# A decoder trunk in exact f32: both column pairs of the MLP's last down group by seven products

## The chip, the cores and the metric

The kernel is one program on one core of a Trainium2 chip. The metric is the device time of one execution in microseconds (us), lower being better. The profile is one execution taken by the hardware profiler; its engines are PE (TensorE), DVE (VectorE), ACT (ScalarE), POOL (GpSimd) and SP (SyncE), the last issuing most transfers.

## The reference

`x` is 256 tokens by 2048. Layer 0 has differential attention, layer 1 latent attention; each is followed by attention into 256 memory tokens and by a squared-ReLU MLP with 8192 hidden columns:

```
def sq_relu_mlp(h, wup, wdown):
    return jnp.square(jax.nn.relu(h @ wup)) @ wdown
...
        a = (p[:, :, 0] - lam * p[:, :, 1]).astype(v.dtype)
        return jnp.einsum('bhqk,bkhd->bqhd', a, v)
...
    for i in range(DEPTH):
...
        x = x + sq_relu_mlp(rms_norm(x, mlp_norm[i]), mlp_wup[i], mlp_wdown[i])
    return rms_norm(x, final_norm)
```

`wup` is 2048 x 8192 and `wdown` 8192 x 2048 in each layer; everything is float32. `a` is the difference of two softmaxes (the second function above stands in the differential attention).

## The kernel before

**Weights.** A weight tile is 128 x 2048 floats (1 MB) and covers 512 rows by 512 columns of a matrix. A plain load puts it into one of seven `raw` tiles. TensorE's fast format holds fewer bits than a float, so each tile is split in two halves of 128x1024: ScalarE casts `raw` to `whi` (line 211), VectorE takes the difference `wlo` (line 212). Four such halves exist at a time, each a pair of `whi` and `wlo`. Activations are split in the same way. Each product is then three matmuls: high by high, low weight by high activation, high weight by low activation (line 164).

**Items.** The MLP's work on TensorE is a list of items. An ordinary *unit* uses one weight tile for both token tiles of 128: 24 matmuls of 128x512 that add into two PSUM banks `mm`. A *chunk* is a list of units with the same output columns; its sums are then added to `x` (line 515) or become hidden values. Hidden columns come in 8 blocks of 1024 (two halves of 512), and a down *group* b multiplies hidden block b with its rows of `wdown`; the output has four column chunks c = 0 to 3.

**Seven products.** A 2 x 2 block product over two token tiles, two weight halves and two column chunks takes eight half-units of 12 matmuls, or seven products p1 to p7 of 12 (banks `pr`), with sums of weight tiles and of activations in place of the eighth. `Seven` does the up projection so for hidden blocks 1 to 7, two depth steps each, 14 items per block. Weight sums are made by VectorE over whole raw tiles (line 837, 42 per layer) and by accumulating transfers of GpSimd (line 829, 14 per layer). `Final` does columns (2, 3) of the last down group by seven products, with two VectorE sums (line 952) and two accumulating transfers (line 949); columns (0, 1) there are four ordinary units. `Pair`, a subclass, does the same for the differential attention's output weights `da_wo` and makes all its weight sums by accumulating transfers, four for each pair.

**Order.** `mlp_line` (line 1089) writes the order of items. It mixes the 98 items of `Seven` with units of the down groups, by estimated VectorE and TensorE cost, into `line` (98 and 64 units in each layer), and sets `end` behind it: the last group, four units and `Final`'s seven products. A job (load and split) runs four items ahead of its matmuls. TensorE's order is that of the program. Around it the code inserts side tasks (softmax, transposes, norms) after a count of TensorE time that a step asks for with `yield`. The orders of VectorE, ScalarE, GpSimd and SP are set by a scheduler. In the differential attention such a step asks for `T_SM + 6.3 + slack` between the softmax of a block and the transposes of `a`, with a slack per head group.

A *seam* below is the place where the MLP's last results are transposed for the next layer's normed input.

Of the kernel before, what the change touches and what calls it, by code (L numbers as in the profile page):

```python
# [17 lines left out]
P = 128  # L18
D = 2048
S = 256  # L20
NT = 2
# [4 lines left out]
MLP_BLOCKS = 8  # L26
SEVEN = (1, 2, 3, 4, 5, 6, 7)
EVS = 7

# [18 lines left out]
def trunk(ctx, tc, x, xT, xT0, mem, memT, positions, gcols, gfinal, lam_vecs, consts, W, out):  # L48
# [121 lines left out]
    def f32(ap):  # L170
        return ap.bitcast(F32)
# [16 lines left out]
    def raw_tile():  # L188
        return wraw.tile([P, 4 * CH], F32, tag="raw", name=nm("raw"))
# [601 lines left out]
    def plan_mlp(l):  # L791
        plan.extend(j for line in mlp_lines[l] for item in line for j in item.jobs)
# [130 lines left out]
    class Final:  # L923

        ORDER = "p1 p2 p5 p6 p3 p7 p4".split()

        def __init__(self, l):
            self.l, self.b = l, MLP_BLOCKS - 1  # L930
            self.cols = (2, 3)
            self.raw = {}
            self.banks = {}
            self.parts = {}
            self.forms = {}

        def source(self, key):
            return W[f"mlp_wdown{self.l}"][8 * self.b + 2 * (1 + key % 10) + key // 10 - 1]

        def fetch(self, key):  # L940
            self.raw[key] = raw_tile()
            load(self.raw[key], self.source(key))

        def home(self, key):
            self.raw[key] = f32(unit()).rearrange("p a k t -> p (a k t)")
            return self.raw[key]

        def onto(self, o, key):
# [5 lines left out]
        def early(self):  # L954
            return [
                lambda hid: (
                    self.sums([k for c in range(2) for k in hid[self.b, c].tasks]),
                    self.fetch(11), load(self.home("t1"), self.source(11)),
                ),
                lambda hid: (self.onto("t1", 12), self.fetch(22), self.fetch(21)),  # L960
                lambda hid: (self.sum("t2", "t1", 22), self.sum("t4", "t2", 21)),
                lambda hid: self.fetch(12),
                lambda hid: self.onto(12, 22),
            ]

        def job(self, p):
            source = {"p1": 11, "p2": 21, "p3": 22, "p4": "t4", "p5": "t1", "p6": "t2", "p7": 12}[p]
            return lambda: halves_of(self.raw[source])

        def items(self):  # L970
            return [Item(self, p, [self.job(p)]) for p in self.ORDER]

# [26 lines left out]
        def products(self, inputs, p, nxt):  # L999
# [21 lines left out]
            for t, j, op in {  # L1021
                "p1": ((0, 0, ALU.add),), "p5": ((1, 1, ALU.add),), "p6": ((0, 1, ALU.subtract),), "p3": ((0, 1, ALU.add),),
                "p7": ((1, 1, ALU.subtract), (1, 0, ALU.add)), "p2": ((0, 0, ALU.add),), "p4": ((1, 0, ALU.add),),
            }[p]:
                xc = xs[t][:, self.cols[j] * CH : (self.cols[j] + 1) * CH]
                with urgent(), behind(added and p == "p7" and added[-1]):
                    summed = nc.vector.tensor_tensor(xc, xc, o, op)
                if p == "p4":
                    added.append(summed)
            done = {"p2": (2, 0), "p3": (3, 0), "p7": (3, 1), "p4": (2, 1)}  # L1030
            if nxt and p in done:
                nxt(*done[p], o)

    class Pair(Final):

        ORDER = "p1 p2 p5 p3 p6 p7 p4".split()
        FETCH = {"p1": ((11, 11), ("t", 12)), "p2": ((21, 21),), "p3": ((22, 22),)}
        STEP = {"p1": ("t", 11), "p5": ("t", 22), "p3": (22, 12), "p6": ("t", 21)}  # L1040
        SPLIT = {"p1": 11, "p2": 21, "p5": "t", "p3": 22, "p6": "t", "p7": 22, "p4": "t"}

        def __init__(self, name, first, cols, forms):
            self.name, self.first, self.cols, self.forms = name, first, cols, forms
            self.raw = {}
            self.banks = {}
            self.parts = {}
            self.steps = []
            self.splits = []

        def source(self, key):
            return W[self.name][4 * self.cols[key % 10 - 1] + self.first + key // 10 - 1]

        def part(self, t, c):
            if not self.parts:
                store = f32(unit()).rearrange("p a k (h t) -> p a (k h) t", t=P)
                self.parts = {(i, j): store[:, i, 4 * j : 4 * j + 4] for i in range(NT) for j in range(2)}
            return self.parts[t, c]

        def job(self, p):  # L1060
            def run():
                for key, at in self.FETCH.get(p, ()):
                    self.raw[key] = raw_tile()
                    load(self.raw[key], self.source(at))
                before = {"p5": ["p1"], "p6": ["p1", "p5"], "p7": ["p3"], "p4": ["p1", "p5", "p6"]}.get(p, [])
                assert all(i in self.steps for i in before)
                self.splits.append(p)
                return halves_of(self.raw[self.SPLIT[p]])

            return run  # L1070

        def items(self, inputs):
            return [Woven(self, p, inputs) for p in self.ORDER]

    class Woven:
# [3 lines left out]
        def step(self):  # L1079
            if self.p in self.of.STEP:  # L1080
                after = {"p5": "p5", "p3": "p3", "p6": "p6"}.get(self.p)
                assert after is None or after in self.of.splits
                self.of.onto(*self.of.STEP[self.p])
                self.of.steps.append(self.p)

        def emit(self):
            self.of.products(self.inputs, self.p, None)

    def mlp_line(l):
# [11 lines left out]
        def down(i):  # L1101

            end = len(groups) - 1
            pairs = ((0, 1), (2, 3)) if (end - i) % 2 == 0 else ((2, 3), (0, 1))
# [21 lines left out]

        rest, after = rest[:-3], rest[-3:]
# [17 lines left out]
        end = down(len(groups) - 1)  # L1145
        for item, step in zip(after + end, end[-1].of.early()):
            item.early = step
        return line + after, end
# [3 lines left out]
    def plan_woven(units, jobs):  # L1152
# [6 lines left out]
    da_pairs = [Pair("da_wo", 0, (c, c + 1), forms) for c in (0, 2)]  # L1159
# [3 lines left out]
        [of.job(p) for of in da_pairs for p in of.ORDER],  # L1163
# [198 lines left out]
    def attention(project, attend, mid, gcol, pairs=()):  # L1362
# [6 lines left out]
        for gi in range(4):  # L1369
# [5 lines left out]
            if pairs and gi == 2:  # L1375
                pairs[0].sums([k for i in first for k in i.tasks])
                weave.extend(k for of in pairs for k in of.items(first))
# [27 lines left out]
    def mlp(l, norm, gnext):  # L1405
# [8 lines left out]
        def out(b, c, t, src, r, wait):  # L1414
# [5 lines left out]
            def task():  # L1420
# [13 lines left out]
        def finish_chunk(of, ps, nxt):  # L1434
            for t in range(NT):
# [3 lines left out]
                else:  # L1439
                    add_residual(t, of.c, ps[t])  # L1440
                    if nxt is not None:
                        nxt(of.c, t, ps[t])
# [6 lines left out]
        def run(line, nxt=None):  # L1449
            for item in line:  # L1450
# [9 lines left out]
                if isinstance(of, Final):  # L1460
                    of.products([hid[of.b, c] for c in range(2)], item.u, nxt)
                    continue
# [10 lines left out]
                if item.u == n - 1 and of.close:  # L1473
                    finish_chunk(of, sums.pop((of.kind, of.c)), nxt)

        line, end = mlp_lines[l]
# [4 lines left out]
        def last(nxt):  # L1481
            free_banks[0] += limit
            run(end, nxt)
# [33 lines left out]
    da_slacks = [0.0, 0.0, 2.0, 0.0]  # L1517
# [298 lines left out]
```

## Time and profile before

| | |
|---|---|
| median of 3 runs | 2211.06 us (2210.5 to 2211.48) |
| the profiled execution's own time | 2209.08 us |
| its span | 2207.3 us |
| mean granted TensorE clock | 0.998 |
| matmuls on TensorE (page) | 10511 |
| VectorE instructions (page) | 2025 |

A group's row gives line, engine, operation, output<-inputs and count; then busy time and mean nanoseconds of one; then the idle time right before them and what ended most of it. A waits row gives the total, how many, and the longest. A row of a window gives its length and each engine's busy time with instruction counts, then the clock, the share of the transfer engines and GB/s. A row in time gives start and duration in us, and in brackets the idle time before it. Matmuls overlap: one of 128x512 lasts 0.39 us, and the next starts 0.23 us after it.

### The profile page before, as it was taken

To read this page: it belongs to the slowest core of one execution; us is meant where nothing else is said; L and a number is where in the kernel's file an instruction comes from. 1 tells how busy PE (TensorE), PEld (TensorE's weight loads), DVE (VectorE), ACT (ScalarE), POOL (GpSimd) and SP (SyncE) were. 2 spreads that over 40 slices of the span, in tenths; PEclk is the share of its full clock that TensorE was granted. 3 is DMA by queue.
4 is the path that set the end of the run, shared out by engine and by line. 5 is a ranking of instruction groups with operands and counts; after the bars stand their busy time and mean duration, and the time that the engine had idled before them with its cause. 6 is when DMAs were issued, how large, how long until landed. Compare 5 with 4: busy or idle time off the path is not lost.

```text
span 2207.3 us, 27663 instructions
## 1 busy us (share of the span) xinstructions
PE 2191.9 (99%) x10511; PEld 1838.4 (83%) x10511; DVE 1814.2 (82%) x2025; ACT 1388.1 (63%) x1855; POOL 147.6 (7%) x230
## 2 busy tenths in 40 slices
PE   9999999999999999999999999999999999999998
PEld 7888888888888888888889988888888888888886
DVE  6665878789889888889886878778988998898888
ACT  7555656666666666666665755656766666666665
POOL 1112210000000000000000411000000000000001
PEclk9999999999999999999999999999999999999999
DMA  9447796436766765865865344634767667677693
GB/s 384 156 155 250 221 268 252 153 124 203 266 204 207 263 203 217 254 214 210 273 213 191 133 155 155 246 134 153 225 232 228 209 249 224 199 258 221 203 297 105
DMA packets 71702, 469.43 MB, mean 213 GB/s; under 512 B 8208, under 2 KB 8592, under 8 KB 17808
## 3 DMA queue, kind: packets, MB, share of 16 engines
q1 hardware_dynamic: 65520, 425.19, 53.5%
q0 software_dynamic: 5760, 41.95, 10.3%
q8 instruction: 82, 1.34, 0.2%
q10 hardware_dynamic: 288, 0.52, 0.1%
q14 instruction: 52, 0.43, 0.1%
HBM read 465.53 MB, written 2.10 MB: 212 GB/s over the span
## 4 chain that ended last, share of the span: by engine, by line
PE 91%; DVE 5%; issue 1%; ACT 1%; DMA 1%; POOL 0%; SPq 0%; DVEq 0%; POOLq 0%; ACTq 0%
PE mm L164 61%; PE pr L164 25%; PE ax L164 2%; DVE wlo L212 2%; PE ax L168 2%; PE mm L168 1%; DVE raw L837 1%; ACT whi L211 1%; DVE unit L459 0%; DVE raw L487 0%; DMA raw<-in_mlp_wup_dram 0%; POOL rs L401 0%; DMA raw<-in_xT_dram 0%; DVE raw L470 0%; DVE x L515 0%
## 5 line engine op out<-in xcount | busy, mean ns | idle before, releaser
L211 ACT CAST whi<-raw 128x1024 fp32r<-128x1024 f32 (+2 forms) x974 | 1012.3, 1041 | 681.4 <-PE mm L164 520.1
L212 DVE TENSOR_TENSOR wlo<-raw,whi 128x1024 fp32r<-128x1024 f32 (+2 forms) x974 | 1161.3, 1210 | 287.7 <-ACT whi L211 272.0
L164 PE MATMUL mm<-whi,unit 128*128 128x512 f32 (+3 forms) x4160 | 1320.7, 389 | 0.6 <-ACT unit L389 0.6
L164 PEld LDWEIGHTS mm<-whi,unit 128*128 128x128 f32 x4160 | 778.0, 188 | 151.5 <-ACT unit L389 2.0
L164 PE MATMUL mm<-wlo,unit 128*128 128x512 f32 (+3 forms) x2080 | 802.8, 386 | 0.9 <-DVE wlo L212 0.8
L164 PE MATMUL pr<-whi,unit 128*128 128x512 f32 x1792 | 579.9, 392 | 0.0
L164 PEld LDWEIGHTS mm<-wlo,unit 128*128 128x128 f32 x2080 | 391.7, 188 | 74.0 <-DVE wlo L212 3.1
L164 PEld LDWEIGHTS pr<-whi,unit 128*128 128x128 f32 x1792 | 336.8, 188 | 69.2
L164 PE MATMUL pr<-wlo,unit 128*128 128x512 f32 x896 | 349.7, 390 | 0.6 <-DVE wlo L212 0.6
L837 DVE TENSOR_TENSOR raw<-raw,raw 128x2048 f32<-128x2048 f32 x84 | 192.3, 2289 | 28.7 <-DMA raw<-in_mlp_wup_dram 28.3
L164 PEld LDWEIGHTS pr<-wlo,unit 128*128 128x128 f32 x896 | 168.5, 188 | 36.0 <-DVE wlo L212 1.8
L829 POOL DMA_DIRECT2D raw<-in_mlp_wup_dram x28 | 24.6, 877 | 1094.8 <-DVE wlo L212 1094.8
L515 DVE TENSOR_TENSOR x<-x,mm 128x512 f32<-128x512 f32 x128 | 84.9, 682 | 3.6 <-PE mm L164 3.4
L401 POOL TENSOR_TENSOR rs<-rs,mhalf 128x1 f32<-128x1 f32 (+1 forms) x26 | 27.5, 1063 | 535.1 <-DVE rs L400 535.1
L356 ACT CAST unit<-ax 128x512 fp32r<-128x512 f32 x68 | 39.4, 582 | 25.7 <-PE ax L168 25.7
L899 DVE TENSOR_TENSOR p<-pr,p 128x512 f32<-128x512 f32 x70 | 47.9, 685 | 2.7 <-PE pr L164 2.7
L357 DVE TENSOR_TENSOR unit<-ax,unit 128x512 fp32r<-128x512 f32 x68 | 46.5, 686 | 1.5 <-ACT unit L356 1.1
L164 PE MATMUL mm<-unit,whi 128*128 128x256 f32 x256 | 47.1, 285 | 0.1
L168 PE MATMUL ax<-identr,p 128*128 128x128 f32 x304 | 46.2, 272 | 0.5 <-ACT unit L1650 0.5
L168 PEld LDWEIGHTS ax<-identr,p 128*128 128x128 f32 x304 | 37.6, 139 | 10.8 <-ACT unit L1650 0.9
L1421 ACT ACTIVATE p<-p,r 128x512 f32<-128x512 f32 x56 | 40.3, 720 | 9.6 <-DVE p L899 9.5
L164 PEld LDWEIGHTS mm<-unit,whi 128*128 128x128 f32 x256 | 40.0, 192 | 0.4 <-DVE unit L357 0.3
(185 smaller groups left out, 1147.0 us busy)
## 6 DMA issues: line engine op xcount, KB each, us to landing
raw<-in_mlp_wup_dram SPq DMA_DIRECT2D x128, 1024.0 KB, 4.9
raw<-in_mlp_wdown_dram SPq DMA_DIRECT2D x128, 1024.0 KB, 5.1
raw<-in_da_wqkv_dram SPq DMA_DIRECT2D x45, 1024.0 KB, 7.3
raw<-in_mlp_wup_dram POOLq DMA_DIRECT2D x28, 1024.0 KB, 8.2
raw<-in_da_wo_dram SPq DMA_DIRECT2D x16, 1024.0 KB, 6.8
raw<-in_ca_wkv_dram SPq DMA_DIRECT2D x16, 1024.0 KB, 5.0
raw<-in_mla_wo_dram SPq DMA_DIRECT2D x16, 1024.0 KB, 5.0
raw<-in_da_wo_dram POOLq DMA_DIRECT2D x8, 1024.0 KB, 10.6
```

What stands on the lines that cost most here:

```text
L164: return nc.tensor.matmul(o, stationary, moving, start=start, stop=stop, skip_group_check=onto)
L168: nc.tensor.transpose(o, src, ident)
L211: nc.scalar.copy(hi, r)
L212: nc.vector.tensor_tensor(lo, r, f32(hi), ALU.subtract)
L356: nc.scalar.copy(hi, src)
L357: nc.vector.tensor_tensor(dst[:, 1, :n, t * P : (t + 1) * P], src, f32(hi), ALU.subtract)
L401: nc.gpsimd.tensor_tensor(r[:, :n], r[:, :n], mhalf.broadcast_to([P, n]), ALU.pow)
L515: nc.vector.tensor_tensor(xc, xc, ps, ALU.add)
L829: tc.keep_in_program_order(nc.gpsimd.dma_start(onto, src, accum_op=ALU.add))
L837: nc.vector.tensor_tensor(o, o, q, ALU.add)
L899: nc.vector.tensor_tensor(o, p, q, op)
L1421: nc.scalar.activation(r, src, AF.Relu, scale=rstd[t])
```

## The change

`Final` goes, and `Pair` is generalised: both column pairs of the last down group, A = (0, 1) and B = (2, 3), are done by seven products. Each pair takes four loads and four accumulating transfers and no VectorE sum of weights. The order of `end` is written out by hand in `CLOSING`; it has the 14 products and 12 ordinary units (`u`), which are those of group 6 and of group 5's columns 2 and 3. These units leave `line`, which keeps 98 items of `Seven` and 52 units. The activations of a product that needs one token tile wait for that tile alone. The step of the last head group of the differential attention is 1.5 longer.

```diff
+LAST = MLP_BLOCKS - 1
+CLOSING = "u u A1 u A2 u B1 u A5 B2 u B5 A6 u A3 u B6 u B3 u A7 u A4 u B7 B4"
...
-    class Final:
...
-        ORDER = "p1 p2 p5 p6 p3 p7 p4".split()
...
-        def sum(self, o, a, b):
-            nc.vector.tensor_tensor(self.home(o), self.raw[a], self.raw[b], ALU.add)
...
+    class Pair:
+        FETCH = {"p1": (11, "t"), "p2": (21,), "p3": (22,)}
+        STEP = {"p1": ("t", 11), "p5": ("t", 22), "p3": (22, 12), "p6": ("t", 21)}
+        SPLIT = {"p1": 11, "p2": 21, "p5": "t", "p3": 22, "p6": "t", "p7": 22, "p4": "t"}
...
+        def step(self, p):
+            o, key = self.STEP[p]
+            assert p == "p1" or p in self.splits
             tc.keep_in_program_order(nc.gpsimd.dma_start(self.raw[o], self.source(key), accum_op=ALU.add))
...
-                need(inputs[c].tasks)
+                need(inputs[c].tasks[t : t + 1] if landed else inputs[c].tasks)
...
         def down(i):
...
-            if i == end:
-                first, second = (c.items() for c in chunks)
-                seven = Final(l).items()
-                return [first[0], seven[0], first[1], seven[1], second[0], seven[2], second[1], *seven[3:]]
-            chunks += [Chunk(l, "down", groups[i], c, close=False) for c in pairs[1]]
+            if i < LAST - 2:
+                chunks += [Chunk(l, "down", groups[i], c, close=False) for c in pairs[1]]
...
-        rest = up(0, 1) + [i for b in range(MLP_BLOCKS - 1) for i in down(b)]
+        rest = up(0, 1) + [i for b in range(LAST - 1) for i in down(b)]
...
-        rest, after = rest[:-3], rest[-3:]
...
+        plain = [
+            i
+            for c in range(4)
+            for i in Chunk(l, "down", both(LAST - 1) if c < 2 else both(LAST - 2, *both(LAST - 1)), c).items()
+        ]
+        pairs = {k: Pair(f"mlp_wdown{l}", 8 * LAST, 2, c, forms) for k, c in (("A", (0, 1)), ("B", (2, 3)))}
...
+        put(0, lambda hid: pairs["A"].sums([k for c in range(2) for k in hid[LAST, c].tasks]))
+        for k, of in pairs.items():
+            put(max(0, at[k + "1"] - 3), lambda hid, of=of: of.fetch("t", of.home()))
+            put(at[k + "1"] - 1, lambda hid, of=of: of.step("p1"))
+        for p in ("p5", "p6", "p3"):
+            for k, of in pairs.items():
+                put(at[k + p[1]] - 3, lambda hid, of=of, p=p: of.step(p))
...
-                split(dst, t, pt)
-                if b == end[-1].of.b:
-                    end[-1].of.keep(t, c, pt)
+                if b < LAST or (t, c) != (1, 0):
+                    split(dst, t, pt)
+                if b == LAST:
+                    pair.keep(t, c, pt)
...
-    da_slacks = [0.0, 0.0, 2.0, 0.0]
+    da_slacks = [0.0, 0.0, 2.0, 1.5]
```

How the order moves is shown at three places. The first is VectorE in layer 0's line, at block 7 of the up projection. Rows with two `raw` are the sums of weight tiles; `wlo` rows are splits, two to each item; `unit` rows are splits of activations. Before, from the second split of p5's first depth step: two splits and a sum for an ordinary unit, p5's second step, the next unit with the next sum, and p6.

```order
L212 TENSOR_TENSOR wlo_8533<-raw_8483,whi_8532 128x1024
L212 TENSOR_TENSOR wlo_8553<-raw_8550,whi_8552 128x1024
L837 TENSOR_TENSOR raw_8483<-raw_8483,raw_8604 128x2048
L212 TENSOR_TENSOR wlo_8557<-raw_8550,whi_8556 128x1024
L212 TENSOR_TENSOR wlo_8578<-raw_8548,whi_8577 128x1024
L212 TENSOR_TENSOR wlo_8582<-raw_8548,whi_8581 128x1024
L212 TENSOR_TENSOR wlo_8609<-raw_8606,whi_8608 128x1024
L837 TENSOR_TENSOR raw_8548<-raw_8548,raw_8693 128x2048
L357 TENSOR_TENSOR unit_8418<-ax_8680,unit_8418 128x4x128
L212 TENSOR_TENSOR wlo_8613<-raw_8606,whi_8612 128x1024
```

After, from the first sum, which stands between the two splits of p5's second step (`wlo_8301` is the second of them); then one unit, the second sum, p6, and the third sum between the two splits of p3.

```order
L839 TENSOR_TENSOR raw_8245<-raw_8245,raw_8329 128x2048
L359 TENSOR_TENSOR unit_8138<-ax_8227,unit_8138 128x4x128
L214 TENSOR_TENSOR wlo_8301<-raw_8269,whi_8300 128x1024
L214 TENSOR_TENSOR wlo_8334<-raw_8331,whi_8333 128x1024
L359 TENSOR_TENSOR unit_8138<-ax_8401,unit_8138 128x4x128
L214 TENSOR_TENSOR wlo_8338<-raw_8331,whi_8337 128x1024
L839 TENSOR_TENSOR raw_8269<-raw_8269,raw_8384 128x2048
L214 TENSOR_TENSOR wlo_8362<-raw_8245,whi_8361 128x1024
L214 TENSOR_TENSOR wlo_8366<-raw_8245,whi_8365 128x1024
L214 TENSOR_TENSOR wlo_8387<-raw_8329,whi_8386 128x1024
L839 TENSOR_TENSOR raw_8245<-raw_8245,raw_8496 128x2048
L214 TENSOR_TENSOR wlo_8391<-raw_8329,whi_8390 128x1024
```

The sums that stood inside units stand inside products, and nearer together.

The second place is TensorE in the differential attention's last head group. `a` is the difference of softmaxes, `identr` the identity that transposes it, and `mm` the sums of an ordinary unit. Before:

```order
L164 MATMUL mm_3249<-whi_3030,unit_2433 128x512
L164 MATMUL mm_3249<-wlo_3031,unit_2433 128x512
L164 MATMUL mm_3249<-whi_3030,unit_2433 128x512 x2
L164 MATMUL mm_3249<-wlo_3031,unit_2433 128x512
L164 MATMUL mm_3249<-whi_3030,unit_2433 128x512
L168 MATMUL ax_3092<-identr,a_3109 128x128 x2
```

After:

```order
L166 MATMUL mm_3249<-whi_3030,unit_2433 128x512
L166 MATMUL mm_3250<-whi_3030,unit_2433 128x512
L166 MATMUL mm_3250<-wlo_3031,unit_2433 128x512
L166 MATMUL mm_3250<-whi_3030,unit_2433 128x512 x2
L166 MATMUL mm_3250<-wlo_3031,unit_2433 128x512
L166 MATMUL mm_3250<-whi_3030,unit_2433 128x512
L170 MATMUL ax_3092<-identr,a_3109 128x128 x2
```

The two transposes moved behind the six matmuls of the unit's second token tile.

The third place is GpSimd's queue at the end of layer 0's MLP. Before, its last transfers are these (`unit` and `raw` are where the weight sum is kept):

```order
L829 DMA raw_8604<-in_mlp_wup_dram 128x2048
L829 DMA raw_8693<-in_mlp_wup_dram 128x2048
L949 DMA unit_9222<-in_mlp_wdown_dram 128x2048
L949 DMA raw_9356<-in_mlp_wdown_dram 128x2048
L401 TENSOR_TENSOR rs_9742<-rs_9742,mhalf 128x1
```

After (`raw_8857` is pair A's running sum, `raw_8994` pair B's):

```order
L960 DMA raw_8857<-in_mlp_wdown_dram 128x2048
L960 DMA raw_8994<-in_mlp_wdown_dram 128x2048
L960 DMA raw_8857<-in_mlp_wdown_dram 128x2048
L960 DMA raw_8994<-in_mlp_wdown_dram 128x2048
L960 DMA raw_8857<-in_mlp_wdown_dram 128x2048
L960 DMA raw_9250<-in_mlp_wdown_dram 128x2048
L960 DMA raw_8994<-in_mlp_wdown_dram 128x2048
L960 DMA raw_9365<-in_mlp_wdown_dram 128x2048
```

Eight accumulating transfers took the place of two, and the running sums stay in raw tiles.

More of the change, by code (lines that the diff above doesn't have):

```diff
@@ L934, in __init__ @@
             self.parts = {}
-            self.forms = {}
+            self.steps = []
+            self.splits = []
         def source(self, key):
[L938 to L946, printed above, removed]
@@ L966, in job, with fetch @@
-        def job(self, p):
[L967 to L971, printed above, removed]
+            at = 12 if key == "t" else key
+            return W[self.name][self.first + self.stride * self.cols[at % 10 - 1] + at // 10 - 1]
+        def fetch(self, key, home=None):
+            if key not in self.raw:
+                self.raw[key] = raw_tile() if home is None else home
+                load(self.raw[key], self.source(key))
@@ L973, in keep, with part @@
+        def part(self, t, c):
+            if not self.parts:
+                store = f32(unit()).rearrange("p a k (h t) -> p a (k h) t", t=P)
+                self.parts = {(i, j): store[:, i, 4 * j : 4 * j + 4] for i in range(NT) for j in range(2)}
+            return self.parts[t, c]
         def keep(self, t, c, src):
@@ L1029, in products @@
                     added.append(summed)
[L1030 to L1073, printed above, removed]
+                if landed:
+                    landed(c, t, o, p in ("p2", "p3", "p7", "p4"))
     class Woven:
@@ L1080, in step @@
             if self.p in self.of.STEP:
[L1081 to L1084, printed above, removed]
+                self.of.step(self.p)
         def emit(self):
-            self.of.products(self.inputs, self.p, None)
+            self.of.products(self.inputs, self.p)
     def mlp_line(l):
```

104 lines of the change are left out of this document (64 added, 40 removed).

## The prediction

> **What bounds the kernel now.** I read the page first, then what TensorE waits for, then the stages, then single places where TensorE stands still.
>
> ```profile
> span 2207.3 us, 27663 instructions
> PE 2191.9 (99%) x10511; PEld 1838.4 (83%) x10511; DVE 1814.2 (82%) x2025; ACT 1388.1 (63%) x1855; POOL 147.6 (7%) x230
> PE 91%; DVE 5%; issue 1%; ACT 1%; DMA 1%; POOL 0%; SPq 0%; DVEq 0%; POOLq 0%; ACTq 0%
> L212 DVE TENSOR_TENSOR wlo<-raw,whi 128x1024 fp32r<-128x1024 f32 (+2 forms) x974 | 1161.3, 1210 | 287.7 <-ACT whi L211 272.0
> L837 DVE TENSOR_TENSOR raw<-raw,raw 128x2048 f32<-128x2048 f32 x84 | 192.3, 2289 | 28.7 <-DMA raw<-in_mlp_wup_dram 28.3
> L211 ACT CAST whi<-raw 128x1024 fp32r<-128x1024 f32 (+2 forms) x974 | 1012.3, 1041 | 681.4 <-PE mm L164 520.1
> PE ax L168 <- DVE a L728: 1.2, 1, 1.2
> PE mm L164 <- DVE wlo L212: 0.8, 2, 0.4
> PE pr L168 <- DVE x L1027: 0.6, 1, 0.6
> PE pr L164 <- DVE wlo L212: 0.6, 2, 0.3
> ```
>
> TensorE (PE) is busy 99% of the span and 91% of the chain that ended last. So fewer matmuls shorten the kernel one for one, as long as VectorE (DVE) delivers the low halves `wlo` in time. VectorE has two large jobs: 974 splits of 1.21 us, and 84 sums of whole weight tiles (line 837, 2.29 us) for the up projection's seven products. Its row shows too that sums wait for loads, 28.3 us in all. ScalarE casts the high halves `whi` in 1.04 us each, and waits for TensorE to free them. The last four rows are TensorE's own waits (total, times, longest): all that splits cost it now is 0.8 + 0.6 = 1.4 us.
>
> ```profile
> core 0: us, PE busy (x) PEld busy (x) DVE busy (x) ACT busy (x) POOL busy (x), PEclk, DMA share, GB/s
> 511.30:1104.00 592.70, 592.01 (x2665) 489.40 (x2664) 520.57 (x464) 384.71 (x421) 13.24 (x15) 1.00 0.71 230
> 1104.00:1165.90 61.90, 61.27 (x286) 50.33 (x285) 54.92 (x62) 40.62 (x56) 0.88 (x1) 1.00 0.63 201
> ```
>
> These are two windows of layer 0's MLP: the long mixed line, and its last part with the down group. TensorE has almost no gap, but VectorE stands at 88% and 89%. It is the engine that gives out first. The granted clock is full.
>
> **Fewer matmuls.** Columns (0, 1) of the last group took four units of 24 matmuls and now take seven products of 12: 96 become 84, in two layers 24 of 128x512 less. The chain of waits gives their pace:
>
> ```profile
> 2119.98 5.44 PE mm L164 x24
> ```
>
> 5.44/24 = 0.227 us each, so 24 of them are **-5.4 us**.
>
> **Two known stalls of TensorE.** The first is in the differential attention, where the transposes of `a` stand before the sum that writes it. The second is at the seam after layer 0's MLP.
>
> ```profile
> 348.61 0.39 PE L164 MATMUL mm<-whi,unit 128*128 128x512 f32 x1
> 350.16 0.44 PE L168 MATMUL ax<-identr,a 128*128 128x128 f32 x2 [1.16 <-DVE a L728]
> 349.64 0.47 DVE L728 SCALAR_TENSOR_TENSOR a<-p,rsum,a 128x256 f32<-128x256 f32 x1
> 1165.90 0.66 PE L168 MATMUL pr<-identr,x 128*128 128x128 f32 x4 [0.63 <-DVE x L1027]
> ```
>
> With the longer step the transposes stand six matmuls (1.36 us) later, and VectorE's rows before `a` stay the same in number. `a` ends at 350.11. TensorE would come to it at 348.61 + 0.23 + 1.36 = 350.20. The stall, 350.16 - 348.61 - 0.23 = 1.32 us, goes: **-1.3**. Next late would be the group's last transposes, for which the order leaves more room. At the seam the last products now have two ordinary units and two products less between the other chunks' sums and the end, so VectorE has fewer sums waiting there. I take the 0.63 off (**-0.6**, between 0 and -0.8 with the gaps just ahead).
>
> **The line without its units.** This is the term that decides. Twelve units go from the line into the end, so the line has 98 product items with 52 units instead of 64. All 42 sums per layer stay in it. A unit's half gives TensorE 12 matmuls (2.72 us) for one split, a product's half 6 matmuls (1.36 us). Counted in VectorE's order, per layer: sums with at least three product halves straight ahead were 2 and become 11. Sums with another sum at most three splits later were 5 and become 12.
>
> What one such sum does, before has once, at 608 us:
>
> ```profile
> 603.62 0.68 DVE L899 TENSOR_TENSOR p<-pr,p 128x512 f32<-128x512 f32 x1
> 604.22 2.35 DVE L212 TENSOR_TENSOR wlo<-raw,whi 128x1024 fp32r<-128x1024 f32 x2
> 606.75 1.23 DVE L212 TENSOR_TENSOR wlo<-raw,whi 128x1024 fp32r<-128x1024 f32 x1 [0.18 <-ACT whi L211]
> 608.01 2.29 DVE L837 TENSOR_TENSOR raw<-raw,raw 128x2048 f32<-128x2048 f32 x1
> 610.22 2.35 DVE L212 TENSOR_TENSOR wlo<-raw,whi 128x1024 fp32r<-128x1024 f32 x2
> 609.57 0.39 PE L164 MATMUL pr<-wlo,unit 128*128 128x512 f32 x1
> 610.71 0.39 PE L164 MATMUL mm<-whi,unit 128*128 128x512 f32 x1
> 611.49 0.50 PE L164 MATMUL mm<-wlo,unit 128*128 128x512 f32 x1 [0.40 <-DVE wlo L212]
> ```
>
> The split that ends at 607.98 is read at 609.57: a spare of 1.6 us, after seven product halves in a row. More than that VectorE can't build there, since only four halves of `whi` and `wlo` exist and a fifth waits for TensorE to read the first. Then come the sum (start to start 2.21) and a split (two take 2.35, the first ends about 611.4; the first row gives 0.60 start to start for an operation of 128x512, which stands between splits too). TensorE was due at 610.71 + 0.23 = 610.94 and got it at 611.49: a stall of 0.55.
>
> As a rule: spare of a half = spare of the one before + TensorE's time on that one - VectorE's work up to its split; below zero it is a stall, and the spare starts from zero again. Where the sum stands inside a unit, this holds too and nothing stalls:
>
> ```profile
> 1025.72 2.36 DVE L212 TENSOR_TENSOR wlo<-raw,whi 128x1024 fp32r<-128x1024 f32 x2 [0.32 <-ACT whi L211]
> 1028.00 2.28 DVE L837 TENSOR_TENSOR raw<-raw,raw 128x2048 f32<-128x2048 f32 x1
> 1030.20 2.35 DVE L212 TENSOR_TENSOR wlo<-raw,whi 128x1024 fp32r<-128x1024 f32 x2
> 1029.39 0.39 PE L164 MATMUL mm<-wlo,unit 128*128 128x512 f32 x1
> 1032.11 0.39 PE L164 MATMUL mm<-wlo,unit 128*128 128x512 f32 x1
> ```
>
> Spare 1029.39 - 1028.08 = 1.31; next 1.31 + 2.72 - (2.20 + 1.14) = 0.69, and the trace agrees (a split that ends about 1031.42, read at 1032.11).
>
> Now block 7 of after, in the order shown with the change. Ahead of the first sum the spare is 1.6 to 2.1. Product half (1.36) against sum, a sum of 128x512 size and split (2.2 + 0.6 + 1.13): 1.6 or 2.1 + 1.36 - 3.93 = a stall of 1.0 or 0.5. Then from zero: +0.23, +0.99 (a unit's half against 0.6 + 1.13) = 1.22; across the second sum -0.61; two product halves +0.23 each = 1.07; third sum inside the next product: 1.07 + 1.36 - 3.33 = -0.90, a stall of 0.9.
>
> I worked the whole line in that way. Ten places per layer go below zero: first half or second of p3 in block 1, dc3's second unit of block 0, p5 of block 4, dc3 of block 2, p4 of blocks 4, 5 and 6, dc0 of block 4, and p5 and p3 of block 7. They add up to 4.5 us where the largest spare is set at 1.76 by its parts, and to 6.3 where it is set so that the measured 0.55 at 611.49 comes out. The same working on before gives 0.3 and 0.55. I take the second, as it meets the nearest row: 6.3 - 0.55, twice, **+11.6**. Upper end: sums already wait for loads (28.3 us), and denser sums need them sooner; with loads landing 1 us later the same working gives 3.5 more per layer. Lower end: 0, if VectorE's order hides more than I reckon; less than -1.4 isn't possible, since the splits cost TensorE no more than that now.
>
> **The end.** Per layer it has 12 units and 14 products (12 x 24 + 14 x 12 = 456 matmuls, 103 us). VectorE has 52 splits and 41 operations of 128x512 there, 52 x 1.14 + 41 x 0.60 = 84 us (81%), no large sum, and by the same working the spare never falls below 1.7: nothing. 20 loads and 8 accumulating transfers run in it, where before ran 2. The attention's pairs have the same mixture and hide it:
>
> ```profile
> 240.00:290.00 50.00, 50.00 (x240) 41.83 (x239) 38.43 (x46) 29.29 (x40) 11.86 (x18) 1.00 0.90 281
> 290.00:340.00 50.00, 50.00 (x236) 41.86 (x235) 39.03 (x47) 31.24 (x45) 8.51 (x15) 1.00 0.83 241
> DMA to landing us min/median/max: 8.0/10.8/13.6
> ```
>
> The last row is of the 12 accumulating transfers of line 949. Tightest is pair A from its fifth product to its sixth, 60 matmuls (13.6 us) apart: the tile is split, added to, and split again. The fifth product's last split is done at about its start (second half at +1.36, read at +0.23 more, spare 1.7). Landing, cast and split from there (10.8 + 1.04 + 1.13) end at 13.0, in time; with 13.6 to landing they end 1.9 late. I take 0.3 per layer, **+0.6** (0 to +3.8). [...] VectorE's net new work (12 splits, 16 adds of 128x512, four 2.29 us sums less) lies in this part, so it is in the 81%.
>
> **Sum.** -5.4 - 1.3 - 0.6 + 11.6 + 0.6 = +4.9. The profiled execution took 2209.1 us (span 2207.3), which gives 2214.0; the runs' median of before is 2211.06, 2.0 above it, so 2216.0.
>
> **Rivals.**
> - The line is not starved: VectorE's splits keep ahead in the dense stretches too. Then all that is left is -7.3 + 0.6, that is 2204.4, faster. For it: VectorE's mean share only rises from 88% to about 90%. Against: at 611.49 one sum was enough. It decides for faster if the line loses less than 1.1 us per layer more than before.
> - The line loses only the places that my lower setting gives, 4.5 - 0.3 per layer: +8.4 instead of +11.6, 2212.8, the same.
> - Transfers come late as well: accumulation stalls at the maximum (+3.8 instead of +0.6), or loads 1 us later (+7): 2219 to 2223. For it: 0.90 DMA share at 281 GB/s in the attention's pairs, and two of seven raw tiles held through the end by the pairs. Against: TensorE lost nothing in those 100 us.
> - The softmax step does not help, since VectorE is late anyway: +1.3, 2217.3.
>
> **How the numbers follow.** A change of 0.2% (4.4 us) is about what a measurement can tell from none, so same is 2206.6 to 2215.5. Line not starved 0.17 (nearly all of it faster); lower setting 0.25 (same); my forecast 0.38, which straddles the upper bound, a quarter of it below; late transfers and the useless step 0.20 (slower). Faster 0.15, same 0.36, slower 0.49. The range leaves out the outer part of both ends: 2206 to 2222; the forecast's own is 2213 to 2219.
>
> **What would show it.** TensorE's waits: `mm` and `pr` on `wlo` grow from 1.4 us to 10 or more, at some ten places per layer, each directly behind a sum line (line 839 then). Block 7's p3 shows 0.9 in both layers. The wait for `a` is gone. The end shows no wait over 1.6 us. If the waits on `wlo` stay under 3 us, the rule for the spare is wrong; if TensorE waits on `raw` transfers or on casts instead, the transfers were the reason.

## The result and the profile after

The changed kernel takes 2224.82 us in the median of 6 runs (2222.04 to 2229.26); before, in runs beside it, 2210.48 us. The ratio is 1.0067, 95% interval 1.0054 to 1.0080: slower by 0.67%. I had forecast slower, but 2216 and no more than 2222. The profiled execution took 2224.6 us, 15.5 more than that of before.

The page of after: span, busy times and chain.

```profile
span 2222.8 us, 27658 instructions
PE 2196.2 (99%) x10487; PEld 1832.2 (82%) x10487; DVE 1824.3 (82%) x2047; ACT 1402.1 (63%) x1865; POOL 155.6 (7%) x242
PE 79%; DVE 11%; DMA 3%; issue 3%; ACT 2%; POOL 1%; DVEq 0%; POOLq 0%; ACTq 0%
```

What TensorE (PE) waits for in after: total, times, longest.

```profile
PE pr L166 <- DVE wlo L214: 6.7, 17, 0.7
PE mm L166 <- DVE wlo L214: 4.5, 7, 1.1
PE mm L166 <- DVE unit L359: 2.4, 2, 1.3
PE ax L170 <- DVE a L730: 2.0, 1, 2.0
```

The 24 matmuls are gone (10487 rows). TensorE's waits for split weights went from 1.4 us to 11.2, at 24 places. VectorE's part of the chain went from 5% to 11%, though its busy share is the same 82%: the average did not show this.

Two windows of layer 0, the line and the end:

```profile
core 0: us, PE busy (x) PEld busy (x) DVE busy (x) ACT busy (x) POOL busy (x), PEclk, DMA share, GB/s
515.00:1068.30 553.30, 547.30 (x2455) 448.21 (x2454) 495.77 (x443) 366.81 (x404) 13.23 (x15) 1.00 0.71 229
1068.30:1174.50 106.20, 106.20 (x486) 87.97 (x485) 85.96 (x98) 65.65 (x80) 6.72 (x8) 1.00 0.85 255
```

The end with its 14 products and eight accumulating transfers has no gap on TensorE at all. The line has 6 us of them, with VectorE at 90%, two points more than before. The mean says little here; what stalls is local. In time, block 7's p3, the place that was worked by hand:

```profile
1008.20 3.49 DVE L214 TENSOR_TENSOR wlo<-raw,whi 128x1024 fp32r<-128x1024 f32 x3
1011.61 2.28 DVE L839 TENSOR_TENSOR raw<-raw,raw 128x2048 f32<-128x2048 f32 x1
1013.81 2.35 DVE L214 TENSOR_TENSOR wlo<-raw,whi 128x1024 fp32r<-128x1024 f32 x2
1013.83 0.61 PE L166 MATMUL pr<-whi,unit 128*128 128x512 f32 x2
1015.08 0.50 PE L166 MATMUL pr<-wlo,unit 128*128 128x512 f32 x1 [0.64 <-DVE wlo L214]
```

TensorE was due at 1014.28 (two matmuls of 0.23 us from 1013.83) and got the split at 1015.08, a stall of 0.80 (the bracket's 0.64 counts from the end of the matmul before); 0.9 had been worked out. A second kind of place, the first unit of down group 3's column chunk 2, has a sum that waits for its load:

```profile
875.59 1.23 DVE L214 TENSOR_TENSOR wlo<-raw,whi 128x1024 fp32r<-128x1024 f32 x1 [0.52 <-ACT whi L213]
879.02 2.29 DVE L839 TENSOR_TENSOR raw<-raw,raw 128x2048 f32<-128x2048 f32 x1 [2.21 <-DMA raw<-in_mlp_wup_dram]
883.70 0.50 PE L166 MATMUL mm<-wlo,unit 128*128 128x512 f32 x1 [0.85 <-DVE wlo L214]
```

And the differential attention, where the wait for `a` moved to the last block:

```profile
354.93 0.34 DVE L729 TENSOR_SCALAR a<-p,rsum 128x256 f32<-128x256 f32 x1
355.59 0.68 DVE L517 TENSOR_TENSOR x<-x,mm 128x512 f32<-128x512 f32 x1
356.98 0.68 DVE L756 TENSOR_TENSOR os<-ax,rs 128x512 f32<-128x512 f32 x1
357.58 0.47 DVE L730 SCALAR_TENSOR_TENSOR a<-p,rsum,a 128x256 f32<-128x256 f32 x1
358.10 0.57 PE L170 MATMUL ax<-identr,a 128*128 128x128 f32 x2 [1.99 <-DVE a L730]
```

```profile
358.30:361.80 3.50, 3.50 (x11) 2.78 (x9) 1.61 (x3) 0.90 (x2) 0.00 (x0) 0.52 0.72 207
```

Between the two operations that write `a` (lines 729 and 730) VectorE now has five others, among them a sum of TensorE's results. The second fence is the window right behind (columns as above): the granted clock is 0.52 there, for 3.5 us.

**Where the 15.5 us are.** I took every gap between starts of matmuls beyond their pace, those over 0.13 us:

| | before | after | difference | forecast |
|---|---|---|---|---|
| layer 0, line | 1.0 | 8.2 | +7.2 | +5.8 |
| layer 1, line | 1.2 | 11.0 | +9.7 | +5.8 |
| last head group (with the slow clock) | 1.3 | 3.8 | +2.5 | -1.3 |
| seam of layer 0 | 0.8 | 0 | -0.8 | -0.6 |
| end, both layers | 0 | 0 | 0 | +0.6 |
| 24 matmuls less | | | -5.4 | -5.4 |

That is +13.2; the rest of the 15.5 lies in gaps under 0.13 us, such as those at TensorE's restart behind each stall (behind p3's the next start comes 0.34 us later in place of 0.23).

### The profile page after: what moved, and what is told of

Read it like the earlier page. It is cut to its first block, busy times and chain, and to the rows that moved or that the text cites. A ratio compares the mean times of both kernels' runs of the same rounds, so it can differ in the third digit from the quotient of the medians.

```text
span 2222.8 us, 27658 instructions
## 1 busy us (share of the span) xinstructions
PE 2196.2 (99%) x10487; PEld 1832.2 (82%) x10487; DVE 1824.3 (82%) x2047; ACT 1402.1 (63%) x1865; POOL 155.6 (7%) x242
## 3 DMA queue, kind: packets, MB, share of 16 engines
q0 software_dynamic: 7488, 54.53, 12.9%
## 4 chain that ended last, share of the span: by engine, by line
PE 79%; DVE 11%; DMA 3%; issue 3%; ACT 2%; POOL 1%; DVEq 0%; POOLq 0%; ACTq 0%
PE mm L166 54%; PE pr L166 20%; DVE wlo L214 6%; DMA raw<-in_mlp_wup_dram 3%; DVE raw L839 2%; PE ax L166 2%; PE ax L170 2%; ACT whi L213 2%; PE mm L170 1%; DVE p L901 0%; DVE unit L359 0%; DVE x L517 0%; DVE unit L461 0%; DVE raw L489 0%; POOL rs L403 0%
## 5 line engine op out<-in xcount | busy, mean ns | idle before, releaser
L213 ACT CAST whi<-raw 128x1024 fp32r<-128x1024 f32 (+3 forms) x998 | 1037.6, 1042 | 682.8 <-PE mm L166 480.6
L214 DVE TENSOR_TENSOR wlo<-raw,whi 128x1024 fp32r<-128x1024 f32 (+3 forms) x998 | 1188.9, 1209 | 299.0 <-ACT whi L213 283.1
L166 PE MATMUL mm<-whi,unit 128*128 128x512 f32 (+3 forms) x4032 | 1281.1, 388 | 2.6 <-DVE unit L359 2.4
L166 PEld LDWEIGHTS mm<-whi,unit 128*128 128x128 f32 x4032 | 754.1, 188 | 150.1 <-DVE unit L359 3.3
L166 PE MATMUL mm<-wlo,unit 128*128 128x512 f32 (+3 forms) x2016 | 778.3, 386 | 4.7 <-DVE wlo L214 4.5
L166 PE MATMUL pr<-whi,unit 128*128 128x512 f32 x1904 | 617.8, 392 | 0.0
L166 PEld LDWEIGHTS mm<-wlo,unit 128*128 128x128 f32 x2016 | 379.7, 188 | 79.5 <-DVE wlo L214 10.0
L166 PEld LDWEIGHTS pr<-whi,unit 128*128 128x128 f32 x1904 | 357.5, 188 | 73.1
L166 PE MATMUL pr<-wlo,unit 128*128 128x512 f32 x952 | 372.9, 392 | 6.8 <-DVE wlo L214 6.7
L839 DVE TENSOR_TENSOR raw<-raw,raw 128x2048 f32<-128x2048 f32 x84 | 192.1, 2286 | 32.0 <-DMA raw<-in_mlp_wup_dram 30.5
L397 ACT ACTIVATE junk<-x 128x512 bf16<-128x512 f32 x56 | 35.1, 627 | 8.7 <-DVE x L1032 5.1
## 6 DMA issues: line engine op xcount, KB each, us to landing
raw<-in_mlp_wdown_dram POOLq DMA_DIRECT2D x16, 1024.0 KB, 11.2
```

The source lines that it names most:

```text
L166: return nc.tensor.matmul(o, stationary, moving, start=start, stop=stop, skip_group_check=onto)
L213: nc.scalar.copy(hi, r)
L214: nc.vector.tensor_tensor(lo, r, f32(hi), ALU.subtract)
L397: return nc.scalar.activation(junk[:, : src.shape[1]], src, AF.Square, scale=scale, accum_out=acc)
L839: nc.vector.tensor_tensor(o, o, q, ALU.add)
```

## The experiments

**The softmax step undone in after, and done alone in before.**

```diff
-    da_slacks = [0.0, 0.0, 2.0, 1.5]
+    da_slacks = [0.0, 0.0, 2.0, 0.0]
```

> The changed kernel with the softmax step of the last head group back at its old length. Theory (the longer step moved the stall from one block's transposes to the next one's and made it longer): the waits for a are 1.2 us again in place of 2.0 us with slow matmuls behind it, 3 to 4 us less than the changed kernel, about 2221. Rival (as predicted, the step saves 1.3): about 2226.

Measured 2220.77 us (2219.02 to 2225.91), 4.0 less than the changed kernel; ratio to before 1.0055 (1.0037 to 1.0072).

```diff
-    da_slacks = [0.0, 0.0, 2.0, 0.0]
+    da_slacks = [0.0, 0.0, 2.0, 1.5]
```

> The kernel before with the longer softmax step alone. Theory: 2 to 3 us slower than before, about 2213, with one wait for a of 2.0 us. Rival (as predicted): 1.3 faster, about 2209.

Measured 2212.10 us (2210.40 to 2215.82), ratio 1.0011 (1.0002 to 1.0021). Its one wait for `a`:

```profile
357.91 0.44 PE L168 MATMUL ax<-identr,a 128*128 128x128 f32 x2 [1.99 <-DVE a L728]
```

Both point the same way: the step saves nothing, as the stall only moves on by one block. Alone it costs 2.0 us, and the interval reaches from 0.4 to 4.6. The 4.0 saved by undoing it is not clear of the noise, since its interval overlaps that of the changed kernel. (The same slack also lengthens the step behind that head group's norm, so the edit is of two steps.) In this profile of the step alone the matmuls behind the same wait of 1.99 us start at the full pace, 0.23 us apart; the last section comes back to it.

**The short line with the old end.**

```diff
-            chunks = [Chunk(l, "down", groups[i], c, open=i == 0) for c in pairs[0]]
+            chunks = [Chunk(l, "down", groups[i], c, open=i in (0, end)) for c in pairs[0]]
...
-            chunks += [Chunk(l, "down", groups[i], c, close=False) for c in pairs[1]]
+            if i < end - 2:
+                chunks += [Chunk(l, "down", groups[i], c, close=False) for c in pairs[1]]
...
-        rest = up(0, 1) + [i for b in range(MLP_BLOCKS - 1) for i in down(b)]
+        rest = up(0, 1) + [i for b in range(MLP_BLOCKS - 2) for i in down(b)]
...
-        rest, after = rest[:-3], rest[-3:]
+        plain = [
+            i
+            for c in range(4)
+            for i in Chunk(l, "down", both(6) if c < 2 else both(5, *both(6)), c).items()
+        ]
+        after = plain[-3:]
...
-        return line + after, end
+        return line + plain, end
```

> The kernel before with the changed kernel's line alone: the same twelve units of each layer leave the line and stand, one after the other, between it and the old end (four units and one pair by seven products). VectorE's order of splits and sums in the line is that of the changed kernel. Theory (the line without its units starves TensorE): 7 us in layer 0 and 10 us in layer 1 more than before, about 2227, with the same waits at the same items as in the changed kernel. Rival (the end's transfers or its pairs cost the time): as before, 2210 to 2212.

Measured 2233.80 us (2230.63 to 2234.99), ratio 1.0107 (1.0092 to 1.0122): 23.7 us more than before, with neither the new pairs nor the longer step in it. TensorE's waits, and then its row at block 7's p3:

```profile
PE mm L164 <- DVE wlo L212: 7.5, 7, 2.5
PE pr L164 <- DVE wlo L212: 5.9, 15, 0.7
PE mm L164 <- DVE unit L357: 2.2, 2, 1.3
```

```profile
1015.65 0.50 PE L164 MATMUL pr<-wlo,unit 128*128 128x512 f32 x1 [0.64 <-DVE wlo L212]
```

The same idle time to a hundredth at p3, and the same three kinds of waits. So the line is the cause. It cost more than the 17 us expected, as two of its sums with a late load stalled TensorE by 2.3 and 2.6 us (the longest wait in the first row is 2.5).

**Four units put back.**

```diff
-            if i < LAST - 2:
-                chunks += [Chunk(l, "down", groups[i], c, close=False) for c in pairs[1]]
+            if i < LAST - 1:
+                chunks += [Chunk(l, "down", groups[i], c, close=i == LAST - 2) for c in pairs[1]]
...
-            for i in Chunk(l, "down", both(LAST - 1) if c < 2 else both(LAST - 2, *both(LAST - 1)), c).items()
+            for i in Chunk(l, "down", both(LAST - 1), c).items()
...
-CLOSING = "u u A1 u A2 u B1 u A5 B2 u B5 A6 u A3 u B6 u B3 u A7 u A4 u B7 B4"
+CLOSING = "u u A1 u A2 u B1 u A5 B2 u B5 A6 A3 u B6 B3 A7 u A4 B7 B4"
```

> The changed kernel with four of the twelve units of each layer put back into the line, so 56 units there and 8 in the end (those of group 6), which needs four more sums of 128x512 on VectorE. Theory (line): about a third of the 17 us comes back, 2219 or less. Rival (end): the pairs' transfers stand closer and wait more, 2225 to 2230.

Measured 2221.95 us (2220.82 to 2222.94), ratio 1.0055 (1.0040 to 1.0070): 2.9 less than the changed kernel, not 5.6, and the two intervals overlap. The waits for split weights fell by more than half, but others took most of that back:

```profile
PE pr L166 <- DVE wlo L214: 3.6, 7, 1.2
PE mm L166 <- DVE unit L359: 3.1, 1, 3.1
PE pr L170 <- DVE x L1032: 1.9, 3, 1.0
PE mm L166 <- DVE wlo L214: 1.5, 4, 0.4
```

11.2 became 5.1 on weights. Counted as in the table, the two lines' gaps fell from 19.2 us to about 5, far more than the third expected. But the 3.1 us wait on a split of activations (line 359) is a new one, at layer 0's seam, and transposes there wait for the sums into `x` (line 1032). With what follows them, the end and the seam of layer 0 have gaps of about 9 us, and layer 1's end 3.6, where the changed kernel had none. So four units more in the line cover most of what it lost, and the end misses them nearly as much. There the rival held: the chain of waits to layer 0's seam goes through an accumulating transfer of 12.25 us, for which ScalarE's next cast waits, and VectorE's work starts late behind it (in layer 1 two such, 13.0 and 12.2 us).

```profile
1144.98 12.25 DMA raw<-in_mlp_wdown_dram
1157.33 1.05 ACT L213 CAST whi<-raw 128x1024 fp32r<-128x1024 f32 x1 [2.21 <-DMA raw<-in_mlp_wdown_dram]
```

**What covers VectorE: more raw tiles, more halves, half the sum.** The room for one more tile comes from the 12 tiles of activations, now 11.

```diff
-RAWS = 7
+RAWS = 8
...
-    units = pool("units", 12)
+    units = pool("units", 11)
```

> The changed kernel with eight raw tiles in place of seven, so that loads start earlier (the room comes from one of the 12 activation tiles). Theory (part of the loss is sums that wait for a load in a dense stretch; the rest is VectorE's own work, which more raw tiles don't change): the idle time of VectorE before its sums falls from 31.9 us to under 5, the four waits of about 1 us behind late loads go (1.0 and 0.95 in layer 0, 0.84, 0.5, 1.2 and 0.9 in layer 1), the waits directly behind sums stay: 4 to 6 us less, 2219 to 2221. Rival (all of the loss is transfers that land late): 12 us less or more, 2212. Rival (loads have no part): 2224 to 2225.

Measured 2222.38 us (2222.03 to 2223.28), ratio 1.0059 (1.0044 to 1.0074), 2.4 less than the changed kernel. VectorE's idle time before sums, and TensorE's row at the wait for `a`:

```profile
DVE raw L839 <- DMA raw<-in_mlp_wup_dram: 17.5, 17, 2.6
```

```profile
360.85 0.44 PE L170 MATMUL ax<-identr,a 128*128 128x128 f32 x2 [3.55 <-DVE a L730]
```

The idle time fell from 30.5 to 17.5 us only, where I had expected nearly all of it to go. The line's gaps fell from 19.2 to 15.0 us, which is what was expected of them, but `a` came 1.6 us later still in the new order, with another slow stretch behind it (a granted clock of 0.58 from 361 to 365 us). The 2.4 us are not clear of the noise, as the two intervals overlap; by the gaps, late loads have a part, the smaller one.

The halves of split weights, five in place of four (also with 11 activation tiles), in before and in after:

```diff
-    whalf = pool("whalf", 4)
-    units = pool("units", 12)
+    whalf = pool("whalf", 5)
+    units = pool("units", 11)
```

> The kernel before with five halves of split weights in place of four (and 11 activation tiles). Theory: VectorE may run one half further ahead; before loses only about 1.5 us in its two lines that way, so 2208 to 2210. Rival (a fifth half helps whatever the line is): 2205 or less.

Measured 2210.19 us (2207.77 to 2213.50), ratio 1.0000 (0.9990 to 1.0009). The waits for `wlo` fell from 1.4 to 0.4 us. Against that stand two waits for sums into `x` (1.1 us) that before does not have; they are in all the profiles here with 11 activation tiles, so the tile that was taken away has a price too.

> The changed kernel with five halves of split weights in place of four (and 11 activation tiles). Theory (four halves cap the spare, so a sum of 2.2 us inside a run of products is not covered): the working of the spare with a fifth half gives 0.8 to 1.1 us of stalls per layer in place of 6.2 to 10, so the waits on wlo fall from 11 us to under 3 and the time by 8 to 12 us, 2213 to 2217. Rival (VectorE's mean share is the limit, there is simply too much work in the line): the stalls only move, 2222 or more.

Measured 2211.96 us (2209.12 to 2217.34), ratio 1.0011 (1.0001 to 1.0021): 12.9 us less than the changed kernel, where the same edit gave before nothing. TensorE's waits:

```profile
PE pr L166 <- DVE wlo L214: 5.1, 6, 2.2
PE ax L170 <- DVE a L730: 3.5, 1, 3.5
```

So VectorE has the time for the line's work; what it lacks is room to run ahead. Six waits are left of 24. The total of 5.1 us is higher than the 3 expected, as waits for loads remain; the profiled execution also took 2217.06 us, 5 above the median.

```diff
-                nc.vector.tensor_tensor(o, o, q, ALU.add)
+                nc.vector.tensor_tensor(o[:, :1024], o[:, :1024], q[:, :1024], ALU.add)
```

> The changed kernel with VectorE's sums of weight tiles taken over 1024 of the 2048 columns, so 1.2 us each in place of 2.3 (this leaves out half of each of the 84 sums). Theory: nearly all waits on wlo behind a sum go, 0.3 to 1.1 us per layer stay, those where a sum waits for its load among them: 10 to 13 us less, 2212 to 2215. Rival (the end's transfers or the waits for loads cost the time): under 4 us less.

Measured 2201.62 us (2199.65 to 2202.25), ratio 0.9963 (0.9948 to 0.9978): 23.2 less than the changed kernel. This kernel leaves out half of each sum, so it shows a cause and is no gain. TensorE's longest waits in it, and VectorE's own before its sums:

```profile
PE ax L170 <- DVE a L730: 2.0, 1, 2.0
PE ax L1198 <- DVE coef L1280: 1.2, 1, 1.2
PE mm L166 <- ACT unit L391: 0.7, 1, 0.7
PE ax L170 <- ACT unit L1646: 0.5, 1, 0.5
```

```profile
DVE raw L839 <- DMA raw<-in_mlp_wup_dram: 24.4, 20, 2.3
```

Not one wait on `wlo` is left, and the line's gaps fall from 19.2 us to none. The sums still wait 24.4 us for loads, and that costs nothing. So a sum's late load need not reach TensorE; here it did where the sum's 2.3 us came on top, in a dense place. (Halved sums also give VectorE some 90 us less to do, by an estimate from 84 sums of 2.29 us and from the 1.2 us of a split, which is half as wide, so this run alone doesn't tell the place of the work from its amount; the five halves, with the same work, do.) This gain was twice what I had expected, since all three kinds of stalls went, not only those directly behind a sum. (The scheduler makes VectorE's order anew for each of these four kernels, so a few places also stand a little differently.)

**Both causes away, and the step made longer still.**

```diff
-    whalf = pool("whalf", 4)
-    units = pool("units", 12)
+    whalf = pool("whalf", 5)
+    units = pool("units", 11)
...
-    da_slacks = [0.0, 0.0, 2.0, 1.5]
+    da_slacks = [0.0, 0.0, 2.0, 0.0]
```

> The changed kernel with five halves of split weights (11 activation tiles) and the softmax step back at its old length: both causes taken away. If they are independent, the five halves save 13 and the step 3 to 4 against the changed kernel: 2207 to 2209, 1 to 3 us faster than before. If the step's 4 us was in the five halves' gain already, 2212.

Measured 2208.38 us (2203.91 to 2214.52, 12 runs), ratio 0.9990 (0.9982 to 0.9999): the one version of this study that computes everything and beats before, by 0.1%, with an interval that just leaves out 1. The two savings add up, 3.6 of the step and 12.9 of the halves. The profile is of the longest of its 12 executions (2214.52). VectorE waits 40.3 us for loads there (4.2 the longest), more than in any other profile here, and one wait of TensorE behind such a sum is 2.7 us long: what is left in the line of this execution are mainly late loads.

```profile
DVE raw L839 <- DMA raw<-in_mlp_wup_dram: 40.3, 28, 4.2
```

```profile
819.23 2.29 DVE L839 TENSOR_TENSOR raw<-raw,raw 128x2048 f32<-128x2048 f32 x1 [1.37 <-DMA raw<-in_mlp_wup_dram]
822.72 0.50 PE L166 MATMUL pr<-wlo,unit 128*128 128x512 f32 x1 [2.71 <-DVE wlo L214]
```

The next kernel has these edits and those of the four units put back:

```diff
-            if i < LAST - 2:
+            if i < LAST - 1:
...
-CLOSING = "u u A1 u A2 u B1 u A5 B2 u B5 A6 u A3 u B6 u B3 u A7 u A4 u B7 B4"
+CLOSING = "u u A1 u A2 u B1 u A5 B2 u B5 A6 A3 u B6 B3 A7 u A4 B7 B4"
```

> As the run with five halves and the old softmax step, with four of the twelve units of each layer put back into the line. If some of the line's stalls are left with five halves (sums that wait for loads), fewer: 2206 to 2208. If the end with 8 units now waits (it had 1.9 us of waits on sums of x with four halves), no better: 2209 to 2211.

Measured 2217.12 us (2216.13 to 2220.02), ratio 1.0032 (1.0020 to 1.0044), 9 us worse than with twelve units at the end. The profile has gaps of 6.3 us in all around layer 0's seam, the longest being:

```profile
1173.16 0.78 PE L166 MATMUL mm<-whi,unit 128*128 128x384 f32 x2 [3.13 <-DVE unit L359]
```

So the end needs units as well, as cover for the transfers, the sums into `x` and the splits of the next layer's input; as with four halves, the chain goes through one accumulating transfer, here of 13.96 us. The profile with twelve units has no gap at this seam, so the 6.3 us can make up most of the difference; the rest was not traced.

The last two lengthen the step, in after with five halves and in before:

```diff
-    da_slacks = [0.0, 0.0, 2.0, 1.5]
+    da_slacks = [0.0, 0.0, 2.0, 4.0]
```

> As the run with five halves, with a softmax step 4.0 longer than the old one. In VectorE's order the two operations that make the last block's a stand near each other again, with no work of later units between them. Theory (what delays a is where the scheduler puts its second operation): no wait for a over 0.5 us, 2206 to 2208, about 1 us less than with the old step. Rival: a still waits 1 to 3.5 us, 2208 to 2212.

Measured 2212.93 us (2210.95 to 2214.42), ratio 1.0011 (1.0002 to 1.0019).

```diff
-    da_slacks = [0.0, 0.0, 2.0, 0.0]
+    da_slacks = [0.0, 0.0, 2.0, 4.0]
```

> The kernel before with the softmax step 4.0 longer and nothing else. Theory: the wait of 1.2 us for a goes and none comes in its place, 2208.8. Rival: it moves again, 2210 to 2213.

Measured 2211.49 us (2208.80 to 2213.75), ratio 1.0003 (0.9994 to 1.0012). In both `a` is late again, in before with the longer step by:

```profile
PE ax L168 <- DVE a L728: 2.0, 1, 2.0
```

With five halves it was 3.0 us. So "no wait" was wrong for both, yet the theory doesn't fall by it. The last block's two operations do stand near each other now, with one other between, and its transposes don't wait. The late `a` is that of the block before. In before with the longer step:

```profile
351.14 0.35 DVE L727 TENSOR_SCALAR a<-p,rsum 128x256 f32<-128x256 f32 x1
351.80 1.22 DVE L212 TENSOR_TENSOR wlo<-raw,whi 128x1024 fp32r<-128x1024 f32 x1
352.93 1.28 DVE L515 TENSOR_TENSOR x<-x,mm 128x512 f32<-128x512 f32 x2
354.12 0.48 DVE L728 SCALAR_TENSOR_TENSOR a<-p,rsum,a 128x256 f32<-128x256 f32 x1
354.66 0.44 PE L168 MATMUL ax<-identr,a 128*128 128x128 f32 x2 [1.99 <-DVE a L728]
```

Its two operations stand 3 us apart, with five others between, a split and two sums among them, and so they do with five halves (353.98 and 356.96). In these two profiles, before's and after's, an `a` that TensorE waits for always has four or five other operations between its two. That agrees with the theory, but no run takes that work away, so it is not shown. Neither longer step (1.5 or 4.0) is better than the old one.

## Why the prediction was wrong

- **Fewer matmuls, -5.4: right.** 24 rows less, at the same pace.
- **The line, +11.6: right in mechanism, too small; measured +17.** The hand-worked p3 of block 7 came out at 0.80 in both layers (0.9 worked out), and all ten named places appear, 4.6 us of stalls in layer 0 and 4.9 in layer 1. That is near the lower setting (4.5), not the higher one (6.3) that I took from one measured stall, so for these places alone the term was too large, and that error hid part of the next. What was missing are stalls of two other kinds. The stalls behind sums that wait for a load in a dense place add up to some 2 us in layer 0 and 4 in layer 1; I had put loads into the upper end only, though the page of before showed 28.3 us of such waits. They are hardly more after (30.5 us), but they stand where nothing covers them. And the splits of the first down group's activations stand in the same queue of VectorE; they came 1.3 and 1.5 us late, a consumer of VectorE that the spare of the weights doesn't count at all.
- **The softmax step, -1.3: wrong in sign.** The first stall did go. I wrote that the next transposes have more room, from TensorE's order alone; VectorE's order shows five operations between the two on the last `a`, where before the second followed the first directly. The wait became 2.0 us, and a granted clock of 0.52 for 3.5 us came on top (about 1.5 us). What brings that part was not shown: with the step alone the same wait had none behind it. "What is late next" was asked and not looked up on the engine that is late.
- **The seam, -0.6: right** (-0.8). **The end, +0.6:** 0; eight accumulating transfers of 7.8 to 13.5 us to landing were hidden, the rival of late transfers there falls, and the end's density was judged rightly. The margin was thin: with 8 units there in place of 12 they reach TensorE.
- **The range.** Its upper end held one of the late loads or the maximum at the end; it needed late loads and the step's wrong sign together, and those two alone are some 10 us. The rival of loads 1 us later (+7) came nearest to the line's missing part.
- **The rivals.** "The line is not starved" falls with the short line alone (+23.7). "The step does not help" held, but it was put at the 1.3 not saved, and the step cost some 2 us more besides.

## What to carry to other kernels

Items that take the bottleneck engine long and the helper engine little are cover; before they are moved away, work out the helper's spare item by item (spare + time on the bottleneck - helper's work), with every job that stands in the helper's queue, not only the one that is watched. A wait that is harmless now, like that of a sum for its load, can stall the bottleneck once its cover is gone. When a stall is moved past, look up in the order of the engine that is late what stands before the next one.

## What was not expected of the hardware

In after, a wait of 1.99 us on TensorE was followed by half the granted clock for 3.41 us: 0.50 in the second row below, with seven matmuls 0.43 us apart in place of 0.23. Behind the same wait of 1.99 us in the kernel with the step alone they start 0.23 us apart, so the length by itself doesn't decide.

The clock of after goes down at 358.27 us, up at 361.68 and down again at 2218.53, behind the last matmul; these times are 3.41 and 1856.85 us apart. Here are stretches of 3.41 us around two waits: the 1.99 us wait in after, and one of 2.87 us, the longer, in the changed kernel with the step undone (columns as above).

```profile
354.86:358.27 3.41, 1.42 (x11) 1.14 (x10) 3.41 (x9) 2.13 (x4) 0.45 (x1) 1.00 0.82 296
358.27:361.68 3.41, 3.41 (x10) 2.73 (x10) 1.64 (x3) 0.78 (x2) 0.00 (x0) 0.50 0.72 204
574.96:578.38 3.42, 1.92 (x9) 1.26 (x7) 3.42 (x4) 1.44 (x2) 0.00 (x0) 1.00 0.12 22
578.38:581.79 3.41, 2.04 (x11) 1.73 (x12) 2.45 (x3) 1.77 (x3) 0.00 (x0) 1.00 0.84 296
581.79:585.20 3.41, 3.41 (x17) 2.79 (x16) 2.92 (x2) 1.73 (x3) 0.00 (x0) 1.00 0.87 305
```

The first wait lies in one stretch (TensorE idle for 1.99 of 3.41 us), and the next stretch has half the clock. The second is shared by two (1.50 and 1.37 idle), and the clock stays at 1.00 behind it. So the longer wait had no slow clock behind it. That the sharing is the reason is a guess from these rows; no run moves a wait to try it, and whether a wait of 2 us costs 1.5 us more could not be told ahead here.
